# A diffusion step on one Trainium2 core: the modulation weights get buffers of their own and GpSimd's DMA queue, and one of three groups on TensorE moves to VectorE

## The chip, the core and the metric

The kernel runs on one core of a Trainium2 chip. The core's engines each work through a queue of their own in order: TensorE (PE: matmuls; its weight loads, PEld, overlap them), VectorE (DVE), ScalarE (ACT), GpSimd (POOL) and SyncE (SP), which here only issues DMAs. They wait for each other by semaphores. Matmuls write to PSUM; all else lies in SBUF.

The metric is the device time of one execution in microseconds, as the median of several. The profile is one execution recorded by the hardware profiler.

## The reference, cut to what matters

A step of a two-layer model on 384 tokens (128 context, 256 latent) of 1024 features. Each layer has three sublayers, an FFN, a mixer and an FFN, so that there are six, numbered s = 0 to 5.

```python
def trunk_layer(x, cond, p, lidx, ctx):
    mod = jax.nn.silu(cond) @ p["w_ada"] + p["b_ada"]      # w_ada: 1024 x 9*1024 in each layer
    mod = mod.reshape(cond.shape[0], 9, 1, 1024)
    h = rmsnorm(x, g[0]) * (1.0 + mod[:, 1]) + mod[:, 0]
    x = x + 0.5 * mod[:, 2] * swiglu(h, w_in[0], w_out[0])     # FFN, hidden 2816
    h = rmsnorm(x, g[1]) * (1.0 + mod[:, 4]) + mod[:, 3]
    m, new_ctx = mixer(h, p, lidx, ctx)     # A differential attention, B gated linear recurrence, C latent attention
    x = x + mod[:, 5] * m
    h = rmsnorm(x, g[2]) * (1.0 + mod[:, 7]) + mod[:, 6]
    x = x + 0.5 * mod[:, 8] * swiglu(h, w_in[1], w_out[1])
```

The line that this case is about is the first: `mod`, the modulation. There are two conditions (one for latent tokens, one for context tokens), so `silu(cond)` is 2 x 1024, and the work of `mod` is to read 18 x 4 MB of `w_ada` once and multiply it by two vectors.

## The kernel before

Activations are held feature-major: eight chunks of 128 features on the partitions, 384 tokens along the row. Every weight is loaded in float32 as a slab `wx` (256 or 512 KB, by SP's queue, L467) and split into a high part `wh` (a cast on ACT, L471) and a low part `wl` (a subtraction on DVE, L472); a product then takes three matmuls (L476 to L478: high by high, high by low, low by high). An FFN goes over 22 hidden chunks f (two products pg and pu for each, then silu and multiplication to `sg`, then its split into `aH` and `aL`), and after that over 16 slabs of the second product `po`. A mixer projects its input (`psw` and others), runs convolution, gates and scans of B, then projects the input of C (`psc`, token-major), normalises it to `cl`, transposes that (`pst`, L992, copied to `cT` on ACT), forms queries and keys (`psq`, `psk`), and attends.

**The modulation.** The first two parts (shift and scale of sublayer 0) are computed at the start (`ada_first`). The other 16 are groups of eight slabs, taken in a fixed order by a stream (`Stream`); each step of the stream takes one slab `adax`, 128 x 1024 floats, 512 KB (`ada_group`, allocation L354, DMA L355). A group is done in one of two ways, by which kind of step opened it. On DVE, a slab takes two multiply-adds, one for each condition (L363; L361 in the first slab of a group), into accumulators with a ring of three buffers, and a group ends with eight matmuls by ones that sum over the partitions (L379). On PE, a slab takes four matmuls (L369) into a bank `adaps`.

Four tables say where the steps stand: `ADA_F[s]` counts the steps on DVE in the two loops of FFN s; `ADA_E[s]` those on PE behind the norm of sublayer s (`norm_stat`); `ADA_M[l]` those on PE between the attention's units of mixer l; and `until` draws what is left over when a modulation is needed.

**What sets the order.** The code is written in a program order and a scheduler places the instructions of each engine by dependency and a priority. Buffers come from pools: a tag is a ring of so many buffers, and a DMA into a buffer waits until its former content was used. Before the change the slabs `adax` share the ring "X" of five buffers with the weight slabs `wx`:

```python
x = wp.tile([P, 1024], F32, name="adax", tag="X")
nc.sync.dma_start(x, w_ada[l, k * P : (k + 1) * P, c0 : c0 + D])
```

Behind a norm, the input of a mixer is known only after a square root; so the first products of `psw` are formed with the raw input `rH`, `rL`, and the normalised `hH`, `hL` come behind. GpSimd's queue holds the small parameters (`late_loads`), the parameters of the mixers, which wait for the silu of chunk 10 of the FFN before (`held`, L773), some outputs, and a few copies.

Of the kernel before, what the change touches and what calls it, by code (L numbers as in the profile page):

```python
# [11 lines left out]
F32 = mybir.dt.float32  # L12
# [3 lines left out]
AX = mybir.AxisListType  # L16
PSUM = bass.MemoryType.PSUM

P = 128
D = 1024  # L20
# [5 lines left out]
T = TC + TL  # L26
# [8 lines left out]
# Slabs of w_ada that each sublayer works through: on the vector engine in the two loops of an FFN, on the tensor  # L35
# engine behind a norm and beside the attention of a mixer.
ADA_F = [[20, 12], None, [22, 8], [17, 16], None, [8, 0]]
ADA_E = [0, 3, 0, 1, 3, 0]
ADA_M = [10, 4]
# Hidden chunks of an FFN that take its input before the norm is known.  # L40
N_RAW = [2, None, 2, 2, None, 2]
# Pairs of output chunks of a mixer whose part of B is computed beside the attention, and behind which of its units.
# [3 lines left out]
# Hidden chunks behind which the small parameters are prepared and those of the mixer are loaded and copied.  # L46
LATE_F = 8
HOLD_LOAD, HOLD_PREP = 10, 16
# Banks that the transposes of a mixer take in turn.
TURN = ["p1", "p2", "p1"]  # L50
# How far ahead of its place the scheduler draws a kind of work.
# [15 lines left out]
def shape_constants():  # L67
    """Identity, ones, and the cosines and signed sines of the rotary, a latent token in a row."""
    grid_w = 64
    t = np.arange(TL)  # L70
    n = 8
    inv = (np.float32(10000.0) ** (-np.arange(n, dtype=np.float32) / np.float32(n))).astype(np.float32)
    row = (t // grid_w).astype(np.float32)
    col = (t % grid_w).astype(np.float32)
    ang = np.concatenate([row[:, None] * inv, col[:, None] * inv], axis=1).astype(np.float32)
    cos = np.cos(ang).astype(np.float32)
    sin = np.sin(ang).astype(np.float32)
    cs = [np.concatenate([a, b], axis=1) for a, b in ((cos, cos), (-sin, sin))]
    rot = np.concatenate([a[q * P : (q + 1) * P] for a in cs for q in range(2)], axis=1)
    return np.ascontiguousarray(  # L80
        np.concatenate([np.eye(P), np.ones((P, P)), rot], axis=1).astype(np.float32), dtype=np.float32
    )
# [3 lines left out]
def hybrid_step_kernel(  # L86
# [40 lines left out]
    nc = tc.nc  # L127
# [3 lines left out]
    wp = ctx.enter_context(tc.tile_pool(name="wp", bufs=5))  # L131
# [6 lines left out]
    # ---------------------------------------------------------------- helpers  # L138
# [55 lines left out]
    # ------------------------------------------------------------- parameters  # L194
# [27 lines left out]
    def late_loads(after):  # L222
        """Loads of what the first sublayer does without, behind those that it waits for."""
# [64 lines left out]
    # --------------------------------------------------------------- adaLN mods  # L288
# [9 lines left out]
    def ada_first(i):  # L298
        """Shift and scale of sublayer 0 for the chunks 2 i and 2 i + 1 of the features."""
# [44 lines left out]
    def ada_group(s, p, on_dve):  # L344
        """Part p (shift, scale, gate) of the modulation of sublayer s, a slab of w_ada in each step."""
# [7 lines left out]
        for k in range(KD):  # L353
            x = wp.tile([P, 1024], F32, name="adax", tag="X")  # L354
            nc.sync.dma_start(x, w_ada[l, k * P : (k + 1) * P, c0 : c0 + D])  # L355
            if on_dve:
                x = x.rearrange("p (h n) -> p h n", h=2)
                for c in range(2):
                    w = sc[:, k, c : c + 1]
                    if k == 0:  # L360
                        ins = V.tensor_scalar(accs[c], x, w, None, op0=ALU.mult)  # L361
                    else:
                        ins = V.scalar_tensor_tensor(accs[c], x, w, accs[c], ALU.mult, ALU.add)  # L363
                    if norm_last["dve"] is not None:
                        behind(ins, norm_last["dve"])
            else:
                x = x.rearrange("p (m a j) -> p a m j", m=KD, a=4)
                for a in range(4):
                    ins = mm(bank[32 * a : 32 * a + 32, 0:256], sc[:, k, :], x[:, a], start=(k == 0), stop=(k == KD - 1))  # L369
                    if norm_last["pe"] is not None:  # L370
                        behind(ins, norm_last["pe"])
            yield
# [22 lines left out]
    class Stream:  # L395
        """Parts of the modulations, computed slab by slab in a fixed order."""
# [27 lines left out]
    # ------------------------------------------------------------------- x^T  # L424
# [3 lines left out]
    @placed("sqacc")  # L428
    def square_acc(k, x=None):
        """Sum of squares over the chunks; those of the last two are added on the tensor engine."""  # L430
        x = xT[:, k, :] if x is None else x
        if k == 0:
            acc["t"] = TT("acc", "acc")
            act(acc["t"], x, AF.Square)
            acc["sq"] = [acc["t"]]
            return
        sq = TT("sq", "sq")
        act(sq, x, AF.Square)
        if k < KD - 2:
            V.scalar_tensor_tensor(acc["t"], sq, EPS * KD / (KD - 3), acc["t"], ALU.add, ALU.add)  # L440
        else:
            acc["sq"].append(sq)
# [8 lines left out]
    # --------------------------------------------------------- weights, splits  # L451
# [9 lines left out]
    def wslab(pieces, nk, ncol, key):  # L461
        """pieces: (dram rows [nk*128, n], column offset). Returns the two parts [128, nk, ncol]."""
# [18 lines left out]
    def rsqrt_newton(v, n, scale, z):  # L481
        """1 / sqrt(v * scale): table value and one Newton step; z: scratch [128, n]."""
# [7 lines left out]
    def load_table(func):  # L490
        """Have the scalar engine take the table of func before it is waited for."""
        act(tab, tab, func)

    @placed("nstat")
    def norm_stat(s):
# [3 lines left out]
        if s:  # L499
            ada.step(ADA_E[s])  # L500
# [4 lines left out]
    def mod_chunk(s, k, r):  # L505
        """The two parts of (x * scale * r) + shift of chunk k."""
# [16 lines left out]
    def raw_chunk(s, k):  # L523
        """The two parts of x * scale of chunk k, and of its shift in two more columns."""
# [12 lines left out]
    def raw_shift(ps, m=P):  # L537
        """What the shift adds to a product with the raw parts, a column for each condition."""
# [18 lines left out]
    # ------------------------------------------------------------------- FFN  # L557
# [93 lines left out]
    # ------------------------------------------------- pieces of the mixer  # L651
# [3 lines left out]
    def small_rsqrt(st, n, scale):  # L655
        """1 / sqrt(st[:, 0] * scale) in st[:, 1], as rsqrt_newton does it."""
# [10 lines left out]
    def swapped(x):  # L667
        """x [.., 32] with its halves exchanged, as [.., 2, 16]."""
# [6 lines left out]
    def rotary_tables(l):  # L675
        """Gains and rotary in one: for q and k and either tile of latent tokens, [cos | sin] of A and of C."""
# [19 lines left out]
    def gain_rotary(l, kind, t, y, o_c, g, heads, r0):  # L696
        """y [128, heads, n] times its gain; in the tiles of latent tokens its last 32 features are rotated."""
# [15 lines left out]
    def norm_c(l, pc):  # L713
        """[compressed q | compressed kv | rotary key] of each tile of tokens, the first two normalised."""
# [23 lines left out]
    def heads_c(l, kind, srcs):  # L738
        """q (kind 0) or k (kind 1) of C, normalised, for the tiles t of srcs: (t, features, shared rotary key)."""
# [31 lines left out]
    def held(out, in_):  # L771
        """Load of a parameter of the mixer, once half of the sublayer before it is done."""
# [7 lines left out]
    def cache_prep(l):  # L780
        """What the cached context gives of keys and values, before the layer's tokens are there."""
# [37 lines left out]
    # ----------------------------------------------------------------- mixer  # L819
    def mixer(l, r_in, hs):  # L820
# [32 lines left out]
        # ---- B: input of the RG-LRU, convolution  # L853
# [30 lines left out]
        # ---- B: gates and scans  # L884
# [50 lines left out]
        # ---- B: output gate  # L935
# [9 lines left out]
        # ---- A: v, token-major  # L945
# [26 lines left out]
        # ---- C: compressed q and kv and the rotary key, token-major  # L972
# [24 lines left out]
        # ---- C: heads  # L997
# [32 lines left out]
        # ---- attention  # L1030
        # tiles of queries, and the key tiles of each: cache, the two of latent tokens, prompt
# [3 lines left out]
        def softmax(ps, n, i, st):  # L1035
            """exp(s - max) and its sum."""
# [37 lines left out]
        def unit_pv(pair, v_, to, e, qt, k0, k1):  # L1074
            """pair: weights [128 q, keys] of heads 2 e and 2 e + 1 and what they are still to be scaled by, if by
            anything; the products are then token-major, else feature-major."""
# [43 lines left out]
        def features(o, j):  # L1120
            """Chunk j of the features of o (three tiles of tokens), a feature in a partition."""
# [5 lines left out]
        # ---- output projection: the part of B beside the attention, then those of C and A  # L1127
# [25 lines left out]
        # ---- A: q, k, token-major; the parts of a map side by side, so that one product adds the three of theirs  # L1153
# [4 lines left out]
        def stacked(kind, o):  # L1158
            """[high, low, high] of q or [high, high, low] of k for each map, of o [128, 256]."""
# [120 lines left out]
    def late_params(after):  # L1280
        """What the mixers need of their small parameters."""
# [6 lines left out]
        # 8 softplus(-lambda) = 8 (max(-lambda, 0) + log1p(exp(-|lambda|)))  # L1288
# [24 lines left out]
        # -lambda of the differential attention, on every partition  # L1313
# [14 lines left out]
    # -------------------------------------------------------------------- run  # L1328
# [68 lines left out]
```

## Time and profile before

| | before |
|---|---|
| median of 3 runs | 1601.47 us (1600.77 to 1601.63) |
| span of the profiled execution | 1594.6 us |
| PE busy | 1545.0 us (97%) |
| DVE busy | 1093.7 us (69%) |
| ACT busy | 743.2 us (47%) |
| POOL busy | 35.9 us (2%) |
| chain of waits that ended last | PE 86%, DVE 5%, ACT 4%, DMA 4% |

No time of its own is recorded for the profiled execution beside its span; the runs' median lies 6.9 us above that span. Busy time counts what an engine executes; records of PE overlap a little, since matmuls are pipelined. In a timeline, a row's first number is its start, the second its length over all instructions in it, and what stands in brackets is the idle time before it and what ended it. A matmul in plain float32, as those of the slabs are, shows as two records.

### The profile page before, as it was taken

What the parts mean: (1) busy time and instruction counts of PE and PEld (TensorE: products, weight loads), DVE (VectorE), ACT (ScalarE), POOL (GpSimd) and SP (SyncE); (2) the same over time, 40 slices, a digit from 0 to 9 for tenths busy, and PEclk for the clock granted to TensorE, in tenths of its full rate; (3) what the DMA queues carried; (4) which work ended last, traced back from release to release, by engine and by line L of the source; (5) the groups of instructions that cost most, each with busy time, mean ns of one, the idle gap of its engine ahead of it and who ended that gap; (6) DMA issues with size and microseconds to landing.
All of it is one profiled execution on the core that took longest, in us unless ns stands there. A gap on an engine that the chain in (4) does not pass through costs nothing.

```text
span 1594.6 us, 24307 instructions
## 1 busy us (share of the span) xinstructions
PE 1545.0 (97%) x9166; PEld 1444.4 (91%) x9166; DVE 1093.7 (69%) x2052; ACT 743.2 (47%) x1376; POOL 35.9 (2%) x66
## 2 busy tenths in 40 slices
PE   7999999999899999999999999999988899999998
PEld 5999899978668999999999999997867699999998
DVE  5876687667678987576587566977767887544332
ACT  5543332459577633333363333325874865333221
POOL 0201000001000000000000100000000000000000
PEclk9999999999899999999999999999989999999999
DMA  9967576432430576566446575764241045555341
GB/s 293 245 198 194 159 217 218 153 108 71 161 123 28 146 224 198 173 212 195 145 119 203 176 206 171 241 220 133 61 147 63 14 133 158 146 146 155 112 150 34
DMA packets 291034, 249.04 MB, mean 156 GB/s; under 512 B 11553, under 2 KB 273158, under 8 KB 290916
## 3 DMA queue, kind: packets, MB, share of 16 engines
q1 hardware_dynamic: 288656, 243.06, 50.6%
q0 software_dynamic: 1936, 4.22, 1.2%
q8 instruction: 72, 1.18, 0.3%
q14 instruction: 46, 0.38, 0.1%
q10 hardware_dynamic: 324, 0.20, 0.1%
HBM read 245.17 MB, written 2.27 MB: 155 GB/s over the span
## 4 chain that ended last, share of the span: by engine, by line
PE 86%; DVE 5%; ACT 4%; DMA 4%; issue 1%; SPq 0%; ACTq 0%; DVEq 0%
PE po L476 9%; PE po L478 9%; PE po L477 9%; PE pg L476 7%; PE pg L478 7%; PE pu L476 7%; PE pu L478 7%; PE pu L477 7%; PE pg L477 7%; DMA adax<-in_w_ada_dram 3%; PE psw L476 1%; PE psw L477 1%; PE adaps L369 1%; PE psg L894 1%; PE psw L478 1%
## 5 line engine op out<-in xcount | busy, mean ns | idle before, releaser
L471 ACT CAST wh<-wx 128x1024 fp32r<-128x1024 f32 (+2 forms) x332 | 332.1, 1002 | 437.4 <-PE po L477 210.3
L472 DVE TENSOR_TENSOR wl<-wx,wh 128x1024 fp32r<-128x1024 f32 (+2 forms) x332 | 384.3, 1160 | 183.9 <-ACT wh L471 182.5
L363 DVE SCALAR_TENSOR_TENSOR ada<-adax,sc,ada 128x1024 f32<-128x1024 f32 x182 | 228.4, 1280 | 146.6 <-DMA adax<-in_w_ada_dram 146.6
L476 PE MATMUL po<-aH,wh 128*128 128x384 f32 x704 | 239.5, 340 | 0.0
L478 PE MATMUL po<-aH,wl 128*128 128x384 f32 x704 | 237.8, 338 | 0.0
L477 PE MATMUL po<-aL,wh 128*128 128x384 f32 x704 | 237.1, 337 | 0.0
L478 PE MATMUL pg<-hH,wl 128*128 128x384 f32 x640 | 216.3, 338 | 4.3 <-DVE wl L472 4.3
L476 PE MATMUL pg<-hH,wh 128*128 128x384 f32 x640 | 216.8, 339 | 0.0
L476 PE MATMUL pu<-hH,wh 128*128 128x384 f32 x640 | 216.1, 338 | 0.0
L477 PE MATMUL pu<-hL,wh 128*128 128x384 f32 x640 | 215.6, 337 | 0.0
L477 PE MATMUL pg<-hL,wh 128*128 128x384 f32 x640 | 215.5, 337 | 0.0
L478 PE MATMUL pu<-hH,wl 128*128 128x384 f32 x640 | 215.4, 337 | 0.0
L476 PEld LDWEIGHTS po<-aH,wh 128*128 128x128 f32 x704 | 132.4, 188 | 3.5 <-issue 2.1
L477 PEld LDWEIGHTS po<-aL,wh 128*128 128x128 f32 x704 | 132.2, 188 | 0.5 <-issue 0.5
L478 PEld LDWEIGHTS po<-aH,wl 128*128 128x128 f32 x704 | 132.2, 188 | 0.0
L478 PEld LDWEIGHTS pg<-hH,wl 128*128 128x128 f32 x640 | 120.1, 188 | 6.2 <-DVE wl L472 6.2
L476 PEld LDWEIGHTS pg<-hH,wh 128*128 128x128 f32 x640 | 120.1, 188 | 2.5 <-issue 2.1
L477 PEld LDWEIGHTS pg<-hL,wh 128*128 128x128 f32 x640 | 120.2, 188 | 0.0
L477 PEld LDWEIGHTS pu<-hL,wh 128*128 128x128 f32 x640 | 120.2, 188 | 0.0
L478 PEld LDWEIGHTS pu<-hH,wl 128*128 128x128 f32 x640 | 120.2, 188 | 0.0
L476 PEld LDWEIGHTS pu<-hH,wh 128*128 128x128 f32 x640 | 120.0, 188 | 0.0
L455 ACT CAST aH<-sg 128x384 fp32r<-128x384 f32 x88 | 45.0, 512 | 147.3 <-DVE sg L595 145.2
(326 smaller groups left out, 2316.2 us busy)
## 6 DMA issues: line engine op xcount, KB each, us to landing
wx<-in_w_ffn_in_dram SPq DMA_DIRECT2D x352, 256.0 KB, 4.0
adax<-in_w_ada_dram SPq DMA_DIRECT2D x144, 512.0 KB, 4.5
wx<-in_w_ffn_out_dram SPq DMA_DIRECT2D x80, 512.0 KB, 3.9
wx<-in_w_in_dram SPq DMA_DIRECT2D x28, 512.0 KB, 3.7
wx<-in_w_ffn_out_dram SPq DMA_DIRECT2D x16, 256.0 KB, 2.7
wx<-in_w_out_dram SPq DMA_DIRECT2D x8, 512.0 KB, 4.0
wx<-in_w_out_dram SPq DMA_DIRECT2D x16, 256.0 KB, 2.9
wx<-in_w_in_dram SPq DMA_DIRECT2D x8, 352.0 KB, 3.4
```

Source lines behind the costliest of these rows:

```text
L363: ins = V.scalar_tensor_tensor(accs[c], x, w, accs[c], ALU.mult, ALU.add)
L369: ins = mm(bank[32 * a : 32 * a + 32, 0:256], sc[:, k, :], x[:, a], start=(k == 0), stop=(k == KD - 1))
L455: nc.scalar.copy(h, src)
L471: nc.scalar.copy(h[:, 0:nk, 0:ncol], x[:, 0:nk, 0:ncol])
L472: V.tensor_tensor(lo[:, 0:nk, 0:ncol], x[:, 0:nk, 0:ncol], h[:, 0:nk, 0:ncol].bitcast(F32), ALU.subtract)
L476: mm(out, wh, xh, start=first, stop=False)
L477: mm(out, wh, xl, start=False, stop=False)
L478: last_mm[0] = mm(out, wl, xh, start=False, stop=last)
L894: mm(ps[:, 0:TG], wg[:, wi, :], xcs[ch], start=True, stop=True)
```

## The change

The slabs get a ring of their own, of three buffers, and are issued by GpSimd. The step behind the norm is removed with its table. The table of the FFNs grows from 30 steps to 36 in FFN 2 and from 33 to 36 in FFN 3, so that TensorE is left with two groups, those of scale and shift for FFN 2, and group (5, 1) (the scale of FFN 5) falls to DVE; mixer 1 has 14 steps where it had 10, and mixer 2 none. GpSimd's space for DMA descriptors is set to 4096. All other lines of the diff remove comments and docstrings, so that later lines have numbers smaller by one to three.

```diff
-ADA_F = [[20, 12], None, [22, 8], [17, 16], None, [8, 0]]
-ADA_E = [0, 3, 0, 1, 3, 0]
-ADA_M = [10, 4]
+ADA_F = [[20, 12], None, [24, 12], [20, 16], None, [8, 0]]
+ADA_M = [14, 0]
...
         for k in range(KD):
-            x = wp.tile([P, 1024], F32, name="adax", tag="X")
-            nc.sync.dma_start(x, w_ada[l, k * P : (k + 1) * P, c0 : c0 + D])
+            x = wp.tile([P, 1024], F32, name="adax", tag="AX", bufs=3)
+            nc.gpsimd.dma_start(x, w_ada[l, k * P : (k + 1) * P, c0 : c0 + D])
...
             norm_last["pe"] = mm(ps[:, 0:T], cm(C_ONE), sq, start=(n_ == 0), stop=(n_ == len(acc["sq"]) - 1))
-        if s:
-            ada.step(ADA_E[s])
         return rsqrt_newton(ps[:, 0:T], T, 1.0 / D, acc["t"])
...
+    nc = _bacc.Bacc("TRN2", target_bir_lowering=False, num_devices=1, dynamic_dma_scratch_size=4096)
```

TensorE behind the norm of mixer 1, before (psn is the sum of squares, psw the first product of the mixer, rH and rL its raw input, adaps the bank of a modulation):

```order
L498 MATMUL psn<-sq,kc_76 128x384
L369 MATMUL adaps<-adax,sc 32x256
L476 MATMUL psw<-rH,wh 128x386
L369 MATMUL adaps<-adax,sc 32x256
L477 MATMUL psw<-rL,wh 128x386
L369 MATMUL adaps<-adax,sc 32x256
L478 MATMUL psw<-rH,wl 128x386
L369 MATMUL adaps<-adax,sc 32x256
```

The same place after the change:

```order
L497 MATMUL psn<-sq,kc_76 128x384
L475 MATMUL psw<-rH,wh 128x386
L476 MATMUL psw<-rL,wh 128x386
L477 MATMUL psw<-rH,wl 128x386
L475 MATMUL psw<-rH,wh 128x386
L476 MATMUL psw<-rL,wh 128x386
L477 MATMUL psw<-rH,wl 128x386
```

The twelve matmuls of slabs between the raw products are gone; it is the same in mixer 2.

TensorE at the end of psc in mixer 1, before (pst are the transposes of cl, psq the queries of C, psk its keys):

```order
L984 MATMUL psc<-wl,hH 128x352
L369 MATMUL adaps<-adax,sc 32x256 x8
L992 MATMUL pst<-kc_76,cl 128x128
L369 MATMUL adaps<-adax,sc 32x256
L992 MATMUL pst<-kc_76,cl 128x128 x2
```

and after the change:

```order
L981 MATMUL psc<-wl,hH 128x352
L368 MATMUL adaps<-adax,sc 32x256 x18
L989 MATMUL pst<-kc_76,cl 128x128
L368 MATMUL adaps<-adax,sc 32x256 x2
L989 MATMUL pst<-kc_76,cl 128x128
```

Twenty matmuls (five slabs) stand there instead of nine; another twelve have come into psc before it. In mixer 2 there were nine at this place too, and after the change the transposes follow psc at once.

GpSimd after the change, from the last of the small parameters on (ukv and uq are parameters of the mixer; before the change ukv followed dl directly). What stands in brackets is what the instruction waits for:

```order
L226 DMA dl<-in_diff_lambda_dram 128x256 [waits DMASW3_49]
L354 DMA adax<-in_w_ada_dram 128x1024 [waits DMASW4_49,DVE_49]
L354 DMA adax<-in_w_ada_dram 128x1024 [waits DMASW5_49,DVE_49]
...
L354 DMA adax<-in_w_ada_dram 128x1024 [waits DMASW2_49,DVE_49]
L770 DMA ukv<-in_mla_w_ukv_dram 128x512 [waits Activation_49]
L770 DMA uq<-in_mla_w_uq_dram 128x384
L354 DMA adax<-in_w_ada_dram 128x1024 [waits DMASW3_49,DVE_49]
L354 DMA adax<-in_w_ada_dram 128x1024 [waits DMASW4_49,DVE_49]
```

Three slabs are issued at the program's start, ten between dl and ukv, and the fourteenth (number 13, counted from 0) stands behind ukv and uq.

## Rows read from the trace of the kernel before

**Rows 1.** The page's busy line: us, share of the span, instructions.

```profile
PE 1545.0 (97%) x9166; PEld 1444.4 (91%) x9166; DVE 1093.7 (69%) x2052; ACT 743.2 (47%) x1376; POOL 35.9 (2%) x66
```

**Rows 2.** Sums by window: window, length, busy us of each engine, TensorE clock, DMA.

```profile
5.00:50.00 45.00, 38.15 (x374) 27.25 (x375) 29.91 (x90) 24.32 (x55) 0.43 (x1) 1.00 1.02 308
100.00:200.00 100.00, 95.02 (x555) 91.44 (x554) 65.67 (x109) 36.59 (x50) 5.46 (x9) 1.00 0.63 173
356.00:404.00 48.00, 46.00 (x249) 40.12 (x248) 39.21 (x73) 45.49 (x78) 4.61 (x9) 0.96 0.28 78
840.00:1100.00 260.00, 260.00 (x1531) 254.75 (x1530) 183.98 (x240) 91.65 (x130) 5.41 (x9) 1.00 0.65 196
```

**Rows 3.** TensorE's waits by releaser: us in total, times, longest.

```profile
PE adaps L369 <- DMA adax<-in_w_ada_dram: 9.1, 6, 1.9
...
PE pg L478 <- DVE wl L472: 4.3, 5, 2.0
```

**Rows 4.** Timeline of TensorE behind the norm of mixer 1: start, length.

```profile
330.01 0.62 PE L369 MATMUL adaps<-adax,sc 128*32 128x256 f32 x2
...
330.93 0.62 PE L369 MATMUL adaps<-adax,sc 128*32 128x256 f32 x2
...
341.15 0.34 PE L477 MATMUL psw<-rL,wh 128*128 128x386 f32 x1
341.33 0.34 PE L478 MATMUL psw<-rH,wl 128*128 128x386 f32 x1
```

**Rows 5.** Timelines of ScalarE and VectorE at the same place.

```profile
344.71 1.05 ACT L471 CAST wh<-wx 128x1024 fp32r<-128x1024 f32 x1 [7.48 <-PE psw L477]
...
346.10 1.58 DVE L515 SCALAR_TENSOR_TENSOR hL<-ht,md,hH 128x128 fp32r<-128x128 f32 x4 [7.03 <-ACT hH L144]
```

**Rows 6.** Timeline of TensorE at the end of psc in mixer 1.

```profile
409.38 0.64 PE L369 MATMUL adaps<-adax,sc 128*32 128x256 f32 x8 [1.86 <-DMA adax<-in_w_ada_dram]
...
414.51 1.97 PE L992 MATMUL pst<-kc,cl 128*128 128x128 f32 x8
```

**Rows 7.** Timelines of TensorE, VectorE and ScalarE behind psc in mixer 2.

```profile
1189.37 1.06 PE L369 MATMUL adaps<-adax,sc 128*32 128x256 f32 x2 [1.94 <-DMA adax<-in_w_ada_dram]
1190.36 1.97 PE L992 MATMUL pst<-kc,cl 128*128 128x128 f32 x8
...
1186.68 0.97 DVE L726 SCALAR_TENSOR_TENSOR cl<-psc,nst,gains 128x128 f32<-128x128 f32 x3 [0.49 <-ACT cl L144]
...
1191.08 0.48 ACT L994 COPY cT<-pst 128x384 f32<-128x384 f32 x1 [3.52 <-PE pst L992]
```

**Rows 8.** VectorE: two groups of the page, then its timeline in FFN 0.

```profile
L472 DVE TENSOR_TENSOR wl<-wx,wh 128x1024 fp32r<-128x1024 f32 (+2 forms) x332 | 384.3, 1160 | 183.9 <-ACT wh L471 182.5
L363 DVE SCALAR_TENSOR_TENSOR ada<-adax,sc,ada 128x1024 f32<-128x1024 f32 x182 | 228.4, 1280 | 146.6 <-DMA adax<-in_w_ada_dram 146.6
...
59.95 0.55 DVE L456 TENSOR_TENSOR aL<-sg,aH 128x384 fp32r<-128x384 f32 x1
60.42 0.75 DVE L361 TENSOR_SCALAR ada<-adax,sc 128x1024 f32<-128x1024 f32 x1
```

**Rows 9.** SP's waits by releaser: us in total, times, longest.

```profile
SPq L355 <- DVE wl L472: 133.3, 60, 14.7
```

**Rows 10.** GpSimd's issues, then DMA issues: count, KB each, us to landing.

```profile
55.06 0.54 POOL L227 DMA_DIRECT2D rowsC<-in_b_ada_dram  x1
...
60.83 1.12 POOL L227 DMA_DIRECT2D dl<-in_diff_lambda_dram  x1 [0.74 <-DMA rot<-in_consts_dram]
...
wx<-in_w_ffn_in_dram SPq DMA_DIRECT2D x352, 256.0 KB, 4.0
adax<-in_w_ada_dram SPq DMA_DIRECT2D x144, 512.0 KB, 4.5
...
wg<-in_lru_w_gate_dram POOLq DMA_DIRECT2D x4, 256.0 KB, 9.5
...
ukv<-in_mla_w_ukv_dram POOLq DMA_DIRECT2D x2, 256.0 KB, 5.2
```

More of the change, by code (lines that the diff above doesn't have):

```diff
@@ L1377 @@
     from concourse.bass_utils import run_bass_kernel_spmd as _run
-    nc = _bacc.Bacc("TRN2", target_bir_lowering=False, num_devices=1)
+    nc = _bacc.Bacc("TRN2", target_bir_lowering=False, num_devices=1, dynamic_dma_scratch_size=4096)
     arrays, args = {}, []
```

## The prediction, made before the changed kernel was run

> **What bounds the kernel now.** I read the page's busy line first [rows 1]: TensorE (PE) is busy 1545.0 us of the span of 1594.6, so PE is the limit and only 49.6 us of it are idle. A change can win in three ways: take work off PE, close one of its idle stretches, or, in a stretch that another engine sets, let that engine go on earlier. Next came the sums over windows [rows 2], to see which stretch is which. In FFN 3 (840 to 1100 us) PE has no idle time at all, while VectorE (DVE) is busy 183.98 of 260 us. In FFN 0 (100 to 200) PE is idle 4.98 us. In the first part of a mixer (356 to 404) ScalarE (ACT) is busy 45.49 of 48 us and PE idles 2 us: that stretch belongs to ACT. In the first stretch (5 to 50) DMA is full, at 308 GB/s. Then I read PE's waits by releaser [rows 3]: 9.1 us for modulation slabs, 4.3 us for the low parts of weights that DVE makes. Last came PE's timeline at the three places where it multiplies modulation slabs [rows 4, 6, 7].
>
> **The change, part by part.**
>
> *Behind the norms.* Mixers 1 and 2 have 12 matmuls of slabs (3 slabs of 4) between the raw products. In the timeline they alternate one by one with the raw matmuls: from 330.01 the pairs come every 0.92 us (330.01 to 330.93), against 0.18 for a raw matmul alone (341.15 to 341.33) [rows 4]. The 12 of them thus cost 12 × (0.92 − 0.18) = 8.9 us of PE. They also hold back others. ACT's cast needs a buffer that these raw products release, and waits 7.48 us for PE; behind it on ACT stand the high parts of the normalised input, for which DVE waits 7.03 us [rows 5]. The stretch that follows is ACT's, so what counts is how much earlier ACT and DVE go on: up to 7.0 us, the smallest of 8.9, 7.48 and 7.03. I take 6.5, since a few tenths of waiting between ACT and DVE will show in its place. The same alternation of 12 and the same wait stand behind the norm of mixer 2, so both together give −13. Bounds: −17.8 (8.9 each, if the whole of PE's gain comes through) and −6 (if later work of ACT takes half).
>
> *Mixer 2 behind psc.* After the change there is no slab on PE. Before, the last pair of slab matmuls starts at 1189.37 after 1.94 us of waiting for a DMA, and the transposes follow at 1190.36 [rows 7]. Their input cl is done on DVE at 1187.65 (1186.68 + 0.97) and ACT then waits 3.52 us for the transposes. Without slabs eight transposes of 1.97 us run from about 1187.2, and ACT goes on when they end, near 1189.0 rather than 1192.3. I take −3.2, bounds −3.5 and 0.
>
> *Mixer 1 behind psc.* All 16 slabs of two groups stay on PE in this mixer: the 3 from behind the norm are now behind the others. Three (12 matmuls) now stand inside the psc products, five (18 + 2 matmuls) between psc and the transposes, three behind psk, the rest in the attention. Before, the main run of transposes starts 7.0 us after psc's end (409.38 − 1.86 = 407.52, to 414.51), with waits for slabs between [rows 6]. Now those five slabs have three buffers only. The fourth is issued when the first was used, some 0.5 us after psc's end, lands 5.7 us later (below) plus 0.6 for the issue, and with a microsecond for the matmuls behind it the transposes begin some 7.8 us after, +0.8. The 12 matmuls inside psc are 3 × 0.64 = 1.9 us (a slab's 4, shown as 8 records, take 0.64 [rows 6]), and part of that lies in waits for ACT. I take +2, bounds −2 and +5 (that landing at 9.5 us). In the attention one slab is drawn where its buffer has just come free; the chain there goes by other engines, so +0.5, bounds 0 and +3.8 (9.5 − 5.7).
>
> *More on DVE.* One group of 8 slabs goes from PE to DVE, and a slab takes two instructions there, one for each condition: 14 more multiply-adds at 1.280 us [rows 8] are 17.9 us, and two opening multiplications of 0.75 make it 19.4. They lie in FFNs 2 and 3; in the latter DVE has 76 of 260 us free [rows 2] and PE none, so they are hidden as long as DVE keeps its lead of about one and a half chunks. The price without that cover is 19.4 us. On PE the group brings 8 reducing matmuls: 8 × 0.18 = +1.4. Because the accumulators of two groups share three buffers, slabs now come in bursts of 7 or 8, two a chunk, and then none for 3 to 5 chunks. A chunk takes PE 48 matmuls of 0.18 [rows 4], some 8.5 us. In a burst DVE has two slabs (4 × 1.28), two low parts of weights (2 × 1.16) and two operations on the result (2 × 0.55) to do meanwhile [rows 8], 8.5 us: just balanced.
>
> *Own buffers and GpSimd's queue.* Before, a slab and a weight take the same five buffers, and SP issues both in order: SP waits 133.3 us with slabs at its head for DVE's use of weights [rows 9]. DVE in turn waits 146.6 us for slabs [rows 8], and behind DVE PE waits 4.3 us for low parts [rows 3]. With buffers of their own, and a queue that doesn't stand behind weights, slabs come ahead. In FFN 0 that may give back 3.5 of the 4.98 us (bounds −5 and +3).
> What does a slab cost on GpSimd (POOL)? An issue takes 0.54 us beside a busy DVE, 1.12 us in the one case (60.83) in which DVE ran a TENSOR_SCALAR beside it [rows 8, 10]. From issue to landing: 512 KB by SP take 4.5 us, 256 KB by SP 4.0, 256 KB by POOL 5.2 (ukv) or 9.5 (wg, in pieces of 256 bytes) [rows 10]. No row shows 512 KB by POOL. The bounds are 4.5 and 9.5; I take 4.5 + (5.2 − 4.0) = 5.7, since ukv is whole rows as a slab is. With three buffers and 2 × 1.28 us of use on DVE a slab then comes every (0.6 + 5.7 + 2.56) / 3 = 3.0 us, and DVE wants one each 4.2 us in a burst, two a chunk. At a landing of 9.5 supply equals demand: (0.6 + 9.5 + 2.56) / 3 = 4.2.
> Slabs also stand in POOL's queue with the held loads of the mixer, whose first waits for ACT's silu of chunk 10 of the FFN. Slab 13 stands behind it and DVE takes it about a chunk (8.5 us) later, against 5.7 for its landing and 1.7 for the three issues ahead: just in time.
> The Trainium skill, page "SBUF — State Buffer", section "SBUF: two separate sides", says that a DMA of GpSimd needs its descriptors written, and that VectorE locks GpSimd out while it runs certain fast operations, so that such a DMA seems to stand still. The 0.54 us beside a busy DVE speaks against it for most operations, the 1.12 us for it in one. By the rule the landing would go past 9.5, which is the slower rival below; by the trace 5.7.
>
> *The start.* The first three slabs, 1.57 MB, are no longer behind the first weights but are issued as soon as POOL has cleared one tile. The stretch from 5 to 50 us moves 308 GB/s at a full DMA [rows 2]: 1.57 MB / 308 GB/s = 5.1 us later for the first sublayer's loads. I take +4, since before one slab also moved in there; bounds 0 (a hole in the stream takes them) and +5.1.
>
> *Sum.* +4 (start) − 3.5 (FFN 0) − 13 (norms) + 2 + 0.5 (mixer 1) − 3.2 (mixer 2) + 1.4 (reducing matmuls) = −11.8 us. The profiled span of 1594.6 becomes 1582.8. The median of the runs is 1601.47, 6.9 us above the span; I carry that difference along as it is: **1589.7 us**.
>
> **The rivals.**
> *A, slower: slabs by POOL land late.* The place is FFN 0, where DVE has no lead yet. If a slab lands L us after its issue with L over 9.5, a burst of 8 loses 8 × (L − 9.5) / 3 on DVE; at L = 12 that is 6.7 us for each of four bursts, of which about half comes back in the chunks without slabs: +13. With that the start takes its 5.1, mixer 1 waits 6.3 us more for its fourth slab (+8 in all), the attention takes +3.8, and the norms still give −13, mixer 2 −3.2 and the reducing +1.4: +15.1, so 1616.6. It decides from L of about 10.5 on, where the sum crosses the time before. For it: wg's 9.5 us, the 1.12 us issue. Against: ukv's 5.2, and the 0.54 beside a busy DVE.
> *B, no difference: the norm's gain is given back.* ACT is busy 45.49 of 48 us right behind it [rows 2]; if ACT's whole work up to psc, and not PE, has set that stretch, an earlier beginning only makes ACT wait elsewhere, for instance for weights. Then the norms give −2, and the sum is +4 − 3.5 − 2 + 2.5 − 3.2 + 1.4 = −0.8 : 1600.7. Against: ACT itself stands still 7.48 us for PE there [rows 5].
> *C, larger gain.* The start is free, FFN 0 gives all of its 5, the norms 8.9 each, and mixer 1's slabs behind psc are hidden: −5 − 17.8 − 3.2 + 1.4 = −24.6, so 1576.9. For it: the bursts leave DVE free for 3 to 5 chunks. Against: the full DMA of the start.
> *D, that it doesn't do what it says* is true in part: 64 of 96 slab matmuls stay on PE, all in mixer 1, among them the ones for which PE waits. This stands in the sum.
>
> **How the numbers follow.** Forecast 0.50, C 0.14, B 0.18, A 0.18. Within 0.2% (3.2 us, about what a measurement of this kernel tells from no change) lie two thirds of B and a little of A: 0.15. Slower: most of A and a bit of B, 0.17. Faster: the forecast, C and a bit of B, 0.68. The forecast's own range is 1582 to 1597. To hold 8 in 10 it takes in half of C and all of B and the near part of A, where landing is about 10.5: 1579 to 1606.
>
> **What would show it.** Right: raw matmuls at 0.18 us without a break behind the norms, ACT's wait of 7.48 gone in both mixers, first transposes in mixer 2 some 3 us earlier, a slab's landing near 5.7 us, DVE's wait for slabs well under 146.6 us, and PE's first full stretch some 4 us later. Wrong: landings of over 9.5 us with POOL's issues lengthened, PE waits for low parts in FFN 0 over 4.3 us, or a wait of PE for slabs in mixer 1 far over the 9.1 of before [rows 3]; or ACT waiting for weights right behind the norm, which is B.

## The result, and the profile after

The changed kernel takes 1579.51 us (median of 4 runs, 1578.18 to 1580.60), the kernel before beside it 1601.55 us (1600.77 to 1602.02): ratio 0.9872, 95% interval 0.9856 to 0.9888, 22.0 us faster. The forecast was 1589.7 us: the right direction, inside the range of 1579 to 1606, but by its lower end and with little more than half of the gain (11.8 us).

The profiled spans tell a smaller difference: 1594.6 us before, 1578.8 after, 15.8 us. Why the medians differ by 6 us more is a question for the experiments (e1).

The page's busy line after the change (compare [rows 1]), the multiply-adds of the slabs on VectorE [rows 8], their issues on GpSimd, and their way to landing [rows 10]:

```profile
PE 1527.9 (97%) x9118; PEld 1441.2 (91%) x9118; DVE 1113.6 (71%) x2068; ACT 746.6 (47%) x1376; POOL 103.4 (7%) x194
...
L362 DVE SCALAR_TENSOR_TENSOR ada<-adax,sc,ada 128x1024 f32<-128x1024 f32 x196 | 244.2, 1280 | 17.8 <-DMA adax<-in_w_ada_dram 17.4
...
L354 POOL DMA_DIRECT2D adax<-in_w_ada_dram x128 | 68.1, 533 | 892.3 <-DVE ada L360 466.5
...
adax<-in_w_ada_dram POOLq DMA_DIRECT2D x128, 512.0 KB, 4.9
```

PE is busy 17.1 us less, of which the smaller number of slab matmuls is a part. DVE waits 17.4 us for slabs where it waited 146.6. The 128 slabs land 4.9 us after their issue in the median, and an issue takes 0.53 us, so the question of the landing (4.5 to 9.5 in the forecast's bounds) is answered near the lower end. The Trainium skill's rule, in "SBUF — State Buffer", section "SBUF: two separate sides", that VectorE can keep GpSimd from writing descriptors while it runs certain fast operations, had been weighed against this change. In this trace it does not show: the longest of 128 issues took 0.66 us with DVE busy 71% of the time. In a second trace of the same kernel (e7, below) it shows once. There an issue on GpSimd takes 0.74 us and ends 0.12 us behind a TENSOR_SCALAR on DVE that began 0.13 us before it:

```profile
154.47 0.74 POOL L354 DMA_DIRECT2D adax<-in_w_ada_dram  x1 [3.91 <-DMA adax<-in_w_ada_dram]
...
154.34 0.75 DVE L360 TENSOR_SCALAR ada<-adax,sc 128x1024 f32<-128x1024 f32 x1 [0.48 <-DMA adax<-in_w_ada_dram]
```

The 1.12 us of [rows 10], beside a TENSOR_SCALAR too, is not alone either: the same issue takes 0.89 to 1.10 us in e1, e2, e5 and e10, where a TENSOR_SCALAR runs beside it, and 0.56 in the other traces, some of which have one there as well. For the slabs such a meeting is rare, and their median issue stays at 0.53 us.

PE's waits by releaser after (columns as in [rows 3]):

```profile
PE pst L989 <- ACT cl L143: 6.5, 1, 6.5
PE adaps L368 <- DMA adax<-in_w_ada_dram: 6.0, 3, 3.7
...
PE pg L477 <- DVE wl L471: 0.2, 1, 0.2
```

The waits for low parts of weights (4.3 us) are gone but for 0.2. Those for slabs fell from 9.1 to 6.0 only. At the top stands a new one: the transposes of mixer 2 wait 6.5 us for ACT. Sums by window of FFN 0 and of the first part of mixer 1 (as in [rows 2], the second moved with the stretch):

```profile
100.00:200.00 100.00, 100.00 (x591) 98.02 (x590) 69.75 (x115) 38.33 (x52) 10.36 (x18) 1.00 0.67 187
350.00:398.00 48.00, 47.07 (x278) 39.86 (x276) 39.44 (x72) 45.67 (x85) 6.11 (x12) 1.00 0.39 117
```

This part of FFN 0 has no idle time of PE left, and the mixer's stretch looks as it did: ACT 45.67 of 48 us.

**Where the time went.** PE's order differs between the kernels in the modulation's matmuls, hardly elsewhere, so the same matmul can be looked up in both timelines. The lengths of the stretches between such matmuls, in us (the third column is an execution of the experiment e1, whose program is that of before but for one setting that moves nothing on PE):

| stretch, by PE's timeline | before | e1 | after | after − before | after − e1 | forecast |
|---|---|---|---|---|---|---|
| to the first raw product pg | 19.21 | 20.29 | 22.54 | +3.3 | +2.3 | +4 |
| FFN 0, to the norm of mixer 1 | 308.07 | 311.91 | 304.34 | −3.7 | −7.6 | −3.5 |
| norm of mixer 1, to the first product of hH | 19.54 | 19.53 | 10.63 | −8.9 | −8.9 | −6.5 |
| to the last matmul of psc | 60.38 | 60.39 | 60.34 | 0.0 | 0.0 | 0 |
| to psq | 9.07 | 9.23 | 11.24 | +2.2 | +2.0 | +2 |
| attention, to the norm of FFN 2 | 114.52 | 115.16 | 114.17 | −0.4 | −1.0 | +0.5 |
| FFNs 2 and 3 | 571.01 | 571.08 | 572.61 | +1.6 | +1.5 | +1.4 |
| norm of mixer 2 | 19.52 | 19.55 | 10.63 | −8.9 | −8.9 | −6.5 |
| to the last matmul of psc | 60.33 | 60.36 | 60.32 | 0.0 | 0.0 | 0 |
| to psq | 10.47 | 9.27 | 8.99 | −1.5 | −0.3 | −3.2 |
| the rest | 402.5 | 403.4 | 403.0 | +0.5 | −0.4 | 0 |
| span | 1594.6 | 1600.2 | 1578.8 | −15.8 | −21.4 | −11.8 |

Two norms give 17.8 us in either comparison. What differs between the two is above all FFN 0 (3.8 us); the start and mixer 2 behind psc differ by some 1 us each, in opposite directions.

The norm of mixer 1 on PE after (answers [rows 4]):

```profile
328.77 0.91 PE L497 MATMUL psn<-sq,kc 128*128 128x384 f32 x2
329.22 0.63 PE L475 MATMUL psw<-rH,wh 128*128 128x386 f32 x1
329.69 0.34 PE L476 MATMUL psw<-rL,wh 128*128 128x386 f32 x1
329.87 0.34 PE L477 MATMUL psw<-rH,wl 128*128 128x386 f32 x1
...
337.51 0.34 PE L475 MATMUL psw<-hH,wh 128*128 128x384 f32 x1
```

After the last psn the raw products follow without a slab between them, and the first normalised product stands at 337.51 instead of 346.82. ACT at the same place (answers the first of [rows 5]):

```profile
335.02 1.20 ACT L143 ACTIVATE hH<-ht,md 128x128 fp32r<-128x128 f32 x3 [0.81 <-DVE ht L508]
336.12 1.04 ACT L470 CAST wh<-wx 128x1024 fp32r<-128x1024 f32 x1
337.06 1.50 ACT L143 ACTIVATE hH<-ht,md 128x256 fp32r<-128x256 f32 x4
```

The cast that waited 7.48 us waits for nothing now.

The end of psc in mixer 1 (answers [rows 6]), PE:

```profile
397.85 0.32 PE L981 MATMUL psc<-wl,hH 128*128 128x352 f32 x1
398.10 1.50 PE L368 MATMUL adaps<-adax,sc 128*32 128x256 f32 x24
403.27 0.64 PE L368 MATMUL adaps<-adax,sc 128*32 128x256 f32 x8 [3.67 <-DMA adax<-in_w_ada_dram]
405.03 1.07 PE L368 MATMUL adaps<-adax,sc 128*32 128x256 f32 x4 [1.11 <-DMA adax<-in_w_ada_dram]
...
407.43 1.53 PE L989 MATMUL pst<-kc,cl 128*128 128x128 f32 x8
```

Three slabs (24 records) are used at once, and the fourth is waited for 3.67 us, the fifth 1.11: three buffers, as the forecast had it. And mixer 2 (answers [rows 7]), PE, then DVE, then ACT:

```profile
1166.82 0.32 PE L981 MATMUL psc<-wl,hH 128*128 128x352 f32 x1
1173.64 2.38 PE L989 MATMUL pst<-kc,cl 128*128 128x128 f32 x9 [6.50 <-ACT cl L143]
...
1170.97 1.22 DVE L471 TENSOR_TENSOR wl<-wx,wh 128x1024 fp32r<-128x1024 f32 x1
...
1172.57 0.16 DVE L656 TENSOR_TENSOR nst<-nst 128x6 f32<-128x6 f32 x1
...
1173.62 0.97 DVE L723 SCALAR_TENSOR_TENSOR cl<-psc,nst,gains 128x128 f32<-128x128 f32 x3 [0.49 <-ACT cl L143]
...
1170.21 1.28 ACT L143 ACT_TABLE_LOAD   x1
1171.50 0.21 ACT L143 ACTIVATE nst<-nst 128x6 f32<-128x6 f32 x1
```

No slab is left here, and still the transposes begin 6.8 us after psc's last matmul. The statistics (nst) that cl needs pass through ACT first, which is busy with casts and the load of a table (1.28 us) and has them at 1171.7; DVE makes low parts of w_out's weights up to 1172.2 and takes them up at 1172.57.

### The profile page after: what moved, and what is told of

Its sections match the earlier page's. It is cut to its first block, busy times and chain, and to the rows that moved or that the text cites. A ratio compares the mean times of both kernels' runs of the same rounds, so it can differ in the third digit from the quotient of the medians.

```text
span 1578.8 us, 24260 instructions
## 1 busy us (share of the span) xinstructions
PE 1527.9 (97%) x9118; PEld 1441.2 (91%) x9118; DVE 1113.6 (71%) x2068; ACT 746.6 (47%) x1376; POOL 103.4 (7%) x194
## 3 DMA queue, kind: packets, MB, share of 16 engines
q0 software_dynamic: 20368, 71.34, 14.8%
## 4 chain that ended last, share of the span: by engine, by line
PE 88%; DVE 4%; ACT 4%; issue 2%; DMA 1%; POOL 0%; ACTq 0%; DVEq 0%; POOLq 0%
PE po L475 9%; PE po L476 9%; PE po L477 9%; PE pg L475 8%; PE pg L477 8%; PE pg L476 8%; PE pu L475 8%; PE pu L477 8%; PE pu L476 8%; PE psw L476 1%; PE psg L891 1%; PE psw L475 1%; PE psw L477 1%; PE adaps L378 1%; ACT gate L143 1%
## 5 line engine op out<-in xcount | busy, mean ns | idle before, releaser
L362 DVE SCALAR_TENSOR_TENSOR ada<-adax,sc,ada 128x1024 f32<-128x1024 f32 x196 | 244.2, 1280 | 17.8 <-DMA adax<-in_w_ada_dram 17.4
L143 ACT ACTIVATE sg<-pg 128x384 f32<-128x384 f32 x80 | 39.4, 493 | 206.5 <-PE pg L477 206.5
L354 POOL DMA_DIRECT2D adax<-in_w_ada_dram x128 | 68.1, 533 | 892.3 <-DVE ada L360 466.5
```

What stands on the lines that cost most here:

```text
L143: ins = nc.scalar.activation(out, in_, func, **kw)
L354: nc.gpsimd.dma_start(x, w_ada[l, k * P : (k + 1) * P, c0 : c0 + D])
```

## The experiments

### e1: where the six microseconds are

```diff
# the kernel before
-    nc = _bacc.Bacc("TRN2", target_bir_lowering=False, num_devices=1)
+    nc = _bacc.Bacc("TRN2", target_bir_lowering=False, num_devices=1, dynamic_dma_scratch_size=4096)
```

> The kernel before, with the one argument for GpSimd's descriptor space (4096) and nothing else. The medians moved by 22 us, the profiled spans by 15.8 (1594.6 to 1578.8); after the change the time lies 1.8 us above its span, before it lay 6.9 above the one span that is known. Theory 1, the descriptor space costs time outside the span: about 1596.5 us, with spans near 1594.6. Theory 2, the profiled execution of the kernel before was a quicker one than its timed runs: 1601.5 us, with spans about 1.8 below it, near 1599.7. Theory 3, the gap belongs to the kernel before and not to that argument: 1601.5 with spans near 1594.6.

Measured: 1601.68 us against 1599.12 of the kernel before on that chip, ratio 1.0008 (0.9992 to 1.0025). In each of these 24 executions the time lies 1.7 to 1.9 us above its span, in the 14 of the kernel before too. So theory 2 holds: the profiled execution of before (1594.6 + 1.8 = 1596.4 us) was a quick one, 5 us under its timed runs, and the setting costs nothing. The executions spread from 1594 to 1605 us, with the granted clock's mean between 0.985 and 0.994. The trace of e1 shows one of the places:

```profile
40.00:50.00 10.00, 8.45 (x79) 6.14 (x79) 3.82 (x11) 1.27 (x4) 0.00 (x0) 0.66 1.12 315
100.00:200.00 100.00, 94.89 (x539) 92.72 (x538) 63.02 (x104) 35.23 (x49) 5.46 (x9) 0.98 0.65 177
```

In the profiled execution of before the clock is full from 5 to 50 us [rows 2]; here it is 0.66 between 40 and 50, and from 100 to 200 us 0.98, with 5.1 us of idle time of PE. The changed kernel's own trace had that fall as well:

```profile
40.00:42.00 2.00, 0.62 (x2) 0.30 (x2) 1.80 (x5) 1.99 (x5) 0.00 (x0) 1.00 1.09 346
42.00:44.00 2.00, 1.01 (x10) 0.48 (x11) 2.00 (x5) 1.46 (x5) 0.00 (x0) 0.79 1.10 348
44.00:46.00 2.00, 2.00 (x29) 1.48 (x30) 1.89 (x8) 0.83 (x2) 0.00 (x0) 0.50 1.15 322
...
48.00:50.00 2.00, 2.00 (x8) 2.00 (x7) 0.00 (x0) 0.00 (x0) 0.00 (x0) 0.51 1.20 289
50.00:52.00 2.00, 2.00 (x34) 1.49 (x33) 0.00 (x0) 0.06 (x1) 0.00 (x0) 1.00 1.10 280
```

PE is idle for 1.4 of 2 us and then for 1.0 of 2, waiting for its inputs; then the clock is at 0.50 (the lower of the two levels, 1.2 GHz) until about 50 us, and full again. In the traces of before, e2, e4, e6 and e8 it does not fall there, in e1, e5, e7 and e9 it falls alike, in e3 and e10 for half as long. e4 and e9 are one kernel: its FFN 0 stretch takes 301.57 us without the fall and 304.51 with it, so it goes with 2.9 us, and is a matter of the execution, not of the change. What decides it stays open: in e2 PE idles for 1.0 us in each of two such stretches, and the clock stays full.

```profile
38.00:40.00 2.00, 0.97 (x7) 0.47 (x6) 2.00 (x5) 1.76 (x5) 0.00 (x0) 1.00 1.08 346
40.00:42.00 2.00, 0.98 (x32) 0.80 (x28) 2.00 (x8) 0.00 (x0) 0.00 (x0) 1.00 1.10 351
```

So the pair of the changed kernel and e1, both with the fall, is nearer to like with like: 21.4 us, beside 22.0 by the medians. It is not quite like. In e1 the clock falls once more in FFN 0, behind a wait of 2.2 us of PE for DVE that the change takes away (psv, see e6):

```profile
115.00:120.00 5.00, 2.77 (x16) 2.39 (x15) 3.57 (x10) 4.15 (x7) 0.00 (x0) 0.92 0.49 122
120.00:125.00 5.00, 5.00 (x23) 5.00 (x23) 4.36 (x19) 1.76 (x3) 0.00 (x0) 0.73 0.61 196
```

### e2: the norm step alone

```diff
# the kernel before
-ADA_E = [0, 3, 0, 1, 3, 0]
-ADA_M = [10, 4]
+ADA_E = [0, 0, 0, 1, 0, 0]
+ADA_M = [13, 7]
```

> The kernel before, but the 3 slabs behind the norm of each mixer are taken between the attention's units of the same mixer instead (13 and 7 steps there); ring, queue and FFN tables as before. By the forecast's term (6.5 us for each norm) less some 2 us in each mixer for the 12 matmuls in their new place: -9, 1592. By the milestones of the two traces (8.9 us for each norm): -14, 1587 to 1588. By the rival in which ScalarE sets the stretch behind the norm: no difference, 1599 to 1602.

Measured: 1584.05 us, ratio 0.9916 (0.9891 to 0.9941) to 1599.12: 13 to 15 us. The norm stretches are 10.60 us each, as after the change, and the stretches behind them 60.31: not a microsecond is given back. The six slabs cost 2.2 us behind psc in mixer 1 and 1.0 in mixer 2 (2.0 and 2.2 beside e1's trace). Two thirds of the change's gain are this one step (0.84% of 1.28%). As a difference it is what the milestones gave, 14 us. Its trace had no fall of the clock (the rows under e1).

### e3: is it the matmuls or the alternation?

```diff
# the kernel before: the raw products of the first chunk, from the second matmul group on, are ordered behind
# the last slab matmul of the norm step
...
+                    for i_ in (i1, i2, i3):
+                        behind(i_, norm_last["grp"])
```

> The kernel before, but the 12 slab matmuls behind the norm of mixers 1 and 2 stand in one row ahead of the raw products instead of alternating with them one by one; nothing else moves. If the alternation is what costs: 12 in a row take 2 to 3 us instead of 11, so 6 us less in each mixer and about 1589 to 1591 us. If each slab matmul costs its 0.74 us wherever it stands: no change, 1601.

Measured: 1584.19 us, ratio 0.9916 (0.9889 to 0.9943). The timeline of PE behind the norm of mixer 1:

```profile
332.02 0.91 PE L499 MATMUL psn<-sq,kc 128*128 128x384 f32 x2
332.87 1.50 PE L369 MATMUL adaps<-adax,sc 128*32 128x256 f32 x24
334.30 0.44 PE L851 MATMUL psw<-rH,wh 128*128 128x386 f32 x1
334.58 0.34 PE L852 MATMUL psw<-rL,wh 128*128 128x386 f32 x1
```

The 12 matmuls (24 records) are done in 1.43 us when they stand in a row, 0.12 each. Alternating with raw products they cost 0.74 each [rows 4]. The norm stretch is 12.25 us, against 19.53 alternating and 10.63 without them: 7.3 of the 8.9 us are the price of the alternation, 1.6 that of the work.

A part of this price can be read from the traces of before. The four matmuls of a slab write to four separate quarters of the bank's partitions (`bank[32 * a : 32 * a + 32, 0:256]`). Standing together, all four (8 records) take 0.64 us [rows 6]; one alone (2 records) takes 0.62 [rows 4]. So the four go on side by side, and one that stands alone between raw products has no company. By this reading a factor of about four of the six is the lost company, and the rest goes with the change from one kind of matmul to the other. No run alternates whole slabs (four matmuls, then a raw product), which would separate the two.

### e5 and e6: the ring or the queue?

```diff
# e5: the changed kernel
-            nc.gpsimd.dma_start(x, w_ada[l, k * P : (k + 1) * P, c0 : c0 + D])
+            nc.sync.dma_start(x, w_ada[l, k * P : (k + 1) * P, c0 : c0 + D])
# e6: the kernel before
-            nc.sync.dma_start(x, w_ada[l, k * P : (k + 1) * P, c0 : c0 + D])
+            nc.gpsimd.dma_start(x, w_ada[l, k * P : (k + 1) * P, c0 : c0 + D])
...
-    nc = _bacc.Bacc("TRN2", target_bir_lowering=False, num_devices=1)
+    nc = _bacc.Bacc("TRN2", target_bir_lowering=False, num_devices=1, dynamic_dma_scratch_size=4096)
```

> The changed kernel, but the slabs are issued by SP again, in their own ring of three: the buffers without the queue. If the buffers alone close the idle time of FFN 0: no wait of TensorE for low parts between 60 and 200 us, and, since SP issues the first slabs behind the first weights, no delay of the start, so 1575 to 1578 us. If the queue is needed: SP's head waits with a slab for VectorE and holds the weights behind it, FFN 0 shows 3 to 5 us of waits for low parts again, 1582 to 1586.

> The kernel before, but the slabs are issued by GpSimd, still in the ring of five that they share with the weights (and with the smaller descriptor space); tables and norm step as before. If the shared ring made FFN 0 wait: no gain, the waits of VectorE for slabs stay over 100 us, 1597 to 1603. If SP's queue made it wait: FFN 0's idle time goes, 1592 to 1595.

> The changed kernel as it is, on the chip of the three others, as their base. By the theory that executions differ by whether TensorE's clock falls at 40 to 50 us: a time of 1576 to 1581, with the start late by 2 to 3 us beside the kernel before at an equal clock, and by 5 to 6 where the clock falls.

Measured on one chip: e5 1578.80 us (ratio 0.9879, 0.9850 to 0.9907), the changed kernel itself (e7) 1577.58 (0.9869, 0.9842 to 0.9896), e6 1593.38 (0.9973, 0.9957 to 0.9989), the kernel before 1597.12.

The ring alone is as good as ring and queue. In e5's trace FFN 0 takes 304.12 us (e7: 304.24), with no wait of PE for low parts from 60 to 200 us, and the start is not late: the first raw product stands at 19.84, in e7 at 21.65, since SP issues the slabs behind the first weights. What SP loses is the attention of mixer 1, 117.63 us against 114.10, and 2.0 us in that of mixer 2 (116.2 against 114.2), where neither kernel has slabs; that stays unexplained. Who waited for slabs in e5 (us, times):

```profile
  ACT wh L470: 11.1, 6
  PEld adaps L368: 10.0, 4
  DVE ada L362: 9.7, 12
  PE adaps L368: 8.3, 4
```

ACT's casts wait for slabs in the FFNs; in the attention of mixer 1 it is PE that waits for them, twice and 3.8 us together (e7: once, 1.1 us). Behind psc e5 gains 1.4 us (9.91 against 11.29), so in mixer 1 GpSimd's queue gives about 2 us, and at the start it takes about 2. The two medians lie within each other's interval.

The queue alone gave a ratio of 0.9973, some 4 us. Neither theory describes it: VectorE's waits for slabs stay as they were (as by the first), and PE's waits for low parts in FFN 0 go but for 0.2 us (as by the second). DVE's waits over the span, and PE's largest from 60 to 200 us:

```profile
DVE ada L363 <- DMA adax<-in_w_ada_dram: 159.7, 64, 5.5
DVE ada L361 <- DMA adax<-in_w_ada_dram: 24.0, 8, 4.0
```

```profile
PE psv L268 <- DVE vC L272: 2.5, 1, 2.5
```

So most of the 146.6 us for which DVE waited for slabs was not what PE paid for; with slabs out of SP's order the weights come early enough, though DVE waits as long as before. But the wait that is left to PE leads back to a slab: DVE stands 3.80 us for one, and the copy of vC (small parameters that PE turns in psv), further on in its order, comes late.

```profile
108.94 0.76 DVE L361 TENSOR_SCALAR ada<-adax,sc 128x1024 f32<-128x1024 f32 x1 [3.80 <-DMA adax<-in_w_ada_dram]
...
115.18 0.23 DVE L272 COPY vC<-psv 128x72 f32<-128x72 f32 x1
```

This is read from the order; no run moves that copy alone. With a ring of its own (e5) this wait of PE is gone as well. FFN 0 took 306.02 us in e6, in an execution without the fall at 40 to 50 us; of those without it, before has 308.07, e2 306.52, and e4, with ring and queue, 301.57. So the ring closes the larger part.

### e4, e9 and e10: the start

```diff
# the changed kernel: the first three slabs
...
+            if first3:
+                tc.add_manual_dep(ld.ins, norm_last["raw"].ins.name, sync, reason="order of the loads")
```

> The changed kernel, but the first three slabs wait for the same instruction as the small parameters (the end of the raw input of FFN 0, some 50 us) and stand ahead of these in GpSimd's queue. By the theory that the slabs' 1.57 MB delay the start: the raw products start 5 to 6 us earlier and the time is 1574 to 1575. By the rival that VectorE then waits for its first slab and hands the delay on: 1579 to 1580. The rival in which the start is set by something else gives 1579.5 with an unchanged start.

> The changed kernel with its first three slabs held until the end of FFN 0's raw input, timed beside the changed kernel itself (next run). If the early slabs cost the start 2 to 3 us in every execution, as the traces at an equal clock show, this one is 2 to 3 us under the changed kernel: a ratio to the kernel before lower by 0.0013 to 0.002. If the start is made up for later (in FFN 0, where TensorE waits for nothing any more, nothing can make up for it) the two are equal.

> The changed kernel itself, as the base of the held start on the same chip: a ratio of 0.986 to 0.988 to the kernel before, whatever the theory.

Measured: e4 1579.15 us (ratio 0.9874; its profiled execution took 1574.25, the other three 1579.13 to 1579.67); then side by side e9 1577.85 (0.9856, 0.9833 to 0.9879) and the changed kernel (e10) 1579.04 (0.9857, 0.9840 to 0.9874). In the traces the first raw product stands at 19.89 and 20.38 us with the slabs held and at 22.54, 21.65 and 22.64 without, so the early slabs cost the start 2.1 us in the mean (1.3 to 2.8 by pairs). The timed runs don't show it: 1.2 us between the medians, less than the runs of either spread. The best version found is thus no more than equal to the changed kernel.

### e8: the slabs of mixer 1 out of the way

```diff
# e4, and:
-            mm(ps, cT[2][:, t * P : (t + 1) * P], ukv, start=True, stop=True)
+            norm_last["pe"] = mm(ps, cT[2][:, t * P : (t + 1) * P], ukv, start=True, stop=True)
```

> The changed kernel with two edits: the first three slabs wait for the end of FFN 0's raw input, and the slab matmuls of mixer 1 may only stand behind the last product of the keys (psk), so that none is ahead of the transposes behind psc. If the slab waits there (3.7 and 1.1 us) set the transposes: these end 1.5 to 2 us earlier, and the time is 2 to 7 us under that of the changed kernel (the larger figure with the start's). If the slabs only meet the same wait later, in the attention, or alternate there with other matmuls: equal to or up to 5 us over the held start alone.

Measured: 1583.40 us, ratio 0.9906 (0.9875 to 0.9937), some 6 us worse than the changed kernel (e7, on the same chip); the two intervals overlap a little, but every run of e8 is slower than every run of e7. PE at the end of psc; then PE on slabs in the attention of mixer 1, in e8 and in e7:

```profile
391.96 0.32 PE L987 MATMUL psc<-wl,hH 128*128 128x352 f32 x1
398.79 1.52 PE L995 MATMUL pst<-kc,cl 128*128 128x128 f32 x5 [6.51 <-ACT cl L143]
...
400.97:523.41 122.44, 12.64 (x128) 3.42 (x128) 0.89 (x2) 0.97 0.36 116
...
408.09:522.19 114.10, 5.10 (x64) 1.69 (x64) 0.44 (x1) 0.99 0.30 94
```

The transposes do come earlier: from psc to psq it is 9.01 us and not 11.24. But without any slab they still wait 6.51 us for ACT's cl, so slabs cost 2.2 us here, not 4.8. And the attention takes 122.44 us instead of 114.10: all 16 slabs (128 records) stand in it now instead of 8, and PE is busy with them for 12.64 us instead of 5.10. Those that filled the wait behind psc had cost little.

## Why the prediction was right and where it was not

*The norms: mis-sized, −13 forecast, −17.8 measured.* The step worked out 8.9 us of PE for each norm, and 7.0 as what ACT and DVE could go on earlier by, and took 6.5. The 8.9 came through whole: ACT's wait of 7.48 is gone, and the stretch up to psc keeps its 60.3 us (59.0 in mixer 1 of e3 and e6) and so starts as much earlier as PE does. The step that failed is "the stretch that follows is ACT's, so what counts is how much earlier ACT and DVE go on", with their waits as the cap. A wait on an engine is no bound for what the engine can gain: ACT's cast stood 17.4 us behind the norm's first matmul and now stands 9.2 behind it (336.12), so it comes 8.2 us earlier although it had waited only 7.48. In [rows 2], too, PE is busy 46.00 of the 48 us that the step gave to ACT. The sentence on PE's price (12 alternating matmuls, 0.74 us each) was right, and e3 shows it to be the alternation.

*FFN 0: mis-sized, and near its trace by luck.* −3.5 forecast, −3.7 between the two profiles, −7.6 against e1. All of the 4.98 us of idle time goes, not 3.5; between the two profiles the fall of the clock, which only the second has, hides 2.9 us of the gain. Without the fall in either it is −6.5 (308.07 to 301.57 in e4), past the bound of −5. The cause given (slabs and weights in one ring and one order, low parts late) is right by e5 and e6, though either edit alone takes the waits for low parts away; DVE's waits for slabs, from which the step argued, remained in e6, and PE paid for them in one place alone (2.5 us, for vC), which the step does not name. The Sum's step that carried 6.9 us as the distance between span and median failed: only 1.8 us lie outside the span; 5.1 were a quicker execution, and a slower execution, in the one trace that we have of one (e1), loses in FFN 0 what the change then saves. This is the 6.2 us by which the medians differ more than the spans.

*The start:* +4 forecast, +3.3 in the pair, of which the early slabs are some 2.1 (held against not held). The step's price of 5.1 us was for all of a full DMA; what the pair shows beyond that is how executions differ (18.7 to 20.7 us to the first raw product in the traces without early slabs).

*Mixer 2 behind psc: wrong step.* −3.2 forecast, −1.5 in the pair and −0.3 against e1. The wait of 1.94 us for a slab in [rows 7] belonged to that execution; in e1 the last pair follows the first transpose without a wait. "Transposes of 1.97 us run from about 1187.2" took cl's end as fixed in its distance to psc. But PE came to the end of psc 14.8 us earlier and DVE's chain of scans and low parts only 13: cl is ready 7.8 us after psc's last matmul begins where before it was 6.0 [rows 7]. The wait of ACT for transposes became a wait of PE for ACT, 6.5 us. e8 shows the same wait in mixer 1 as soon as the slabs are gone.

*Mixer 1 behind psc* came as forecast in its sum, +2.2 for +2, but by luck. The 12 matmuls inside psc, up to 1.9 us in the step, cost nothing (60.3 us as before), and the transposes begin 9.3 us behind psc's end (407.43 against 398.17) and not 7.8. The step had the wait for the fourth slab but not that for the fifth (1.11 us) with its matmuls between the transposes; and the landing of 4.9 us lay under the 5.7 taken.

*FFNs 2 and 3* came as forecast, +1.6 for +1.4. The 14 more multiply-adds are hidden: FFNs 2 and 3 grew by the 8 reducing matmuls alone. Rival A (late landing) is excluded by the 4.9 us, B by the 60.3 us behind the norms; C's price of 8.9 for each norm and its 5 us in FFN 0 were the right ones, its free start was not.

## What to carry to other kernels

Look at what alternates: a few small matmuls of another kind, put one by one between the products of a busy TensorE, cost six times their price in a row (0.74 against 0.12 us), so filling work should stand in blocks, at least of the matmuls that can go on side by side, best where PE waits anyway. A wait of a second engine for the bottleneck is not a cap on what the second gains; take the bottleneck's own number and then look whether the next stretch keeps its length. And before a term rests on one profiled execution, see how its time stands to the timed runs: the part that is not outside the span belongs to a slower execution and may change with the edit.

## What the runs showed that was not expected

Two executions of one program differ by up to 11 us (1594.11 to 1605.38 in e1), and one place of it is the start: the granted clock falls to the lower level for about 6 us behind two short idle times of PE, in some executions only, and goes with 2.9 us (304.51 against 301.57). Issues of slabs on GpSimd took 0.53 us at the median; a few were longer, up to 0.99 us (e6), and the longest one of e6, as that of e7, ended 0.12 us behind a TENSOR_SCALAR of VectorE. The queue itself hardly changed a slab's way to landing: in the ring of five it took 4.4 us by GpSimd (e6) and 4.5 by SP (before), in the ring of three 4.9 by GpSimd (e7) and 4.7 by SP (e5).
